# Softmax attention's output product as seven half-size products, in two parts around the linear attention's first half

## The chip, the cores and the metric

The kernel runs on one core of one Trainium2 chip. The metric is the time of one execution on the device, in microseconds (us); the median of 3 runs before the change is 1637.56 us. Engines are named as in the profile: PE is the matrix engine (PEld its weight loads), DVE the vector engine, ACT the scalar engine, POOL the GpSimd engine, and SP the queue from which every DMA of this kernel is issued, in one order.

## The reference

One layer of an encoder block, float32, one batch of 1024 tokens, width 1024:

```python
h = _rms_norm(x, norm_mix_g[l])
proj = h @ w_in[l]
(g_q, g_k, g_v, g_r, g_lr_f, g_lr_b,
 s_q, s_k, s_v, gate_a, gate_b) = jnp.split(proj, split_at, axis=-1)
y_gla = _gla_branch(...) @ w_o_gla[l]      # linear attention, norm, swish gate by g_r
y_swa = _swa_branch(...) @ w_o_swa[l]      # softmax attention in a window of 128
merged = jax.nn.sigmoid(gate_a) * y_gla + jax.nn.sigmoid(gate_b) * y_swa
x = x + merged @ w_out[l]
h2 = _rms_norm(x, norm_ffn_g[l])
gu = h2 @ w_ffn_in[l]
x = x + (jax.nn.silu(gu[..., :D_FF]) * gu[..., D_FF:]) @ w_ffn_out[l]
```

The change concerns `y_swa`'s product with `w_o_swa` (1024 x 1024 by 1024 x 1024 tokens), and the place where the gates `gate_a` and `gate_b` get their factor of the first norm, 1/rms(x) of each token.

## The kernel before

Activations lie with features on the 128 partitions and tokens along the free axis. A tile is 128 x 512: one eighth of the features (index `k` or `m`, 0 to 7) for one half of the tokens (index `s`, 0 or 1). Float32 accuracy comes from splitting each operand into a high part (`h`, rounded by ACT's copy to fp32r) and a low part (`l`, the rest, a subtraction on DVE), and from three matmuls for each 128 x 128 block: high by high, high by low, low by high (`mm3`, and `product` for four blocks in a row). So a half-size product, four blocks deep, is 12 matmuls of 512 columns for each output tile.

Weights come in units of 128 x 512 (four blocks). `wunit` loads one to `wr` (4 buffers), splits it to `wh` on ACT and `wl` on DVE (5 buffers each). `wsplit` does the split alone, for units that are sums of others.

PE's instructions run in the order of the source. The order on DVE, ACT and SP is set by the framework's scheduler: among what it takes to be ready, what comes first in the source goes first. Each of these queues then runs in that fixed order, and an instruction that waits holds up those behind it.

Stages of the time line: projections of the input (0 to 346 us; from 88 us on a part made of seven half-size products per pair of output features, with the gates as its first eight pairs, `pairs[0]` to `pairs[7]`); linear attention (346 to 557 us) and softmax attention (to 740 us), both interleaved with the remaining projections; then the branch products, which the change touches; then the two feed-forward products (from about 1010 us), also by seven half-size products.

The gates' stage: `x_two`, `x_four` and `x_last` make three quarters of each pair's output on DVE (`xc`, `xu`) and hand them to `out_quarter`, which stores them to DRAM (`keep`). The remaining quarter (`ga`, first token half) was stored earlier, by `keep_raw` in `x_first`.

The branch stage before, from 740 us on, in PE's order:

1. `branch_b(0)`: `y_swa`'s product for the first token half, 8 groups of 24 matmuls (`hgroup`), on the split tiles `obh`, `obl` that `prep_b(0)` made during the last of the softmax attention. Each group ends with a product by its gate on DVE, into `xg[m][s]`.
2. `prep_a(0)` (no PE work): for each `k` two DMA loads (`lo`, the linear attention's output, and `lr`, its swish gate's input; two buffers each), a sigmoid on ACT (`sg`, one buffer), two products on DVE, and the split into `oah`, `oal`. `prep_b(1)`: the second half's `ob` tiles.
3. `branch_a(0)`: `y_gla`'s product, 8 groups, each times its gate, plus `xg`, then split into `mh`, `ml`.
4. `branch_b(1)`, `prep_a(1)`.
5. `out_proj(0)`: the product with `w_out` for the first token half, 8 groups; then `branch_a(1)`, and `out_proj(1)`.

`gate` loads a gate's tile, multiplies it by `rstd` on DVE (L1123) and takes the sigmoid on ACT (L1124). PSUM has 8 banks: 4 of tag `mm` and 4 of tag `ch`; before the change all groups of this stage use `mm`.

Of the kernel before, what the change touches and what calls it, by code (L numbers as in the profile page):

```python
# [24 lines left out]
NG = 8  # L25
# [5 lines left out]
def body(tc, i, out):  # L31
    nc = tc.nc
    with ExitStack() as root:
        dram = root.enter_context(tc.tile_pool(name="scr", bufs=1, space=bass.MemoryType.DRAM))
        cst = root.enter_context(tc.tile_pool(name="cst", bufs=1))
        wp = root.enter_context(tc.tile_pool(name="wp", bufs=1))
# [18 lines left out]
        def scratch(name, shape=(P, 512)):  # L55
            return dram.tile(list(shape), F32, tag=name, name=name)
# [21 lines left out]
        def mm3(o, ah, al, bh, bl, start, stop):  # L78
            mm(o, ah, bh, start, False)
            mm(o, ah, bl, False, False)  # L80
            mm(o, al, bh, False, stop)
# [10 lines left out]
        rstd = cst.tile([P, T], F32, tag="rstd", name="rstd")  # L92
# [22 lines left out]
        scr = {}  # L115
# [179 lines left out]
        def wsplit(src, n):  # L295
            h = wp.tile([P, n], FR, tag="wh", name=nm("wh"), bufs=5)
            l = wp.tile([P, n], FR, tag="wl", name=nm("wl"), bufs=5)
            nc.scalar.activation(h, src, AF.Copy)  # L298
            nc.vector.tensor_tensor(l, src, h.bitcast(F32), op=ALU.subtract)  # L299
            return h, l  # L300

        def product(o, w, x, nk, start, stop):
            h, l = w
            for kk in range(nk):
                c = slice(kk * P, (kk + 1) * P)
                nc.tensor.matmul(o, h[:, c], x[kk][0], start=start and kk == 0, stop=False, skip_group_check=True)  # L306
                nc.tensor.matmul(o, h[:, c], x[kk][1], start=False, stop=False, skip_group_check=True)  # L307
                nc.tensor.matmul(o, l[:, c], x[kk][0], start=False, stop=kk == nk - 1, skip_group_check=True)  # L308

        def keep(name, s, t):  # L310
            d = scratch(f"{name}_{s}")
            nc.sync.dma_start(out=d[:t.shape[0]], in_=t)
            scr[name, s] = d
# [38 lines left out]
        def out_quarter(F, b, s, t, src=None):  # L352

            if F.scales:
                nc.vector.scalar_tensor_tensor(t, t if src is None else src, F.scales[b], rstd[:, s * HT:(s + 1) * HT],
                                               op0=ALU.mult, op1=ALU.mult)
            elif src is not None:
                nc.scalar.copy(t, src)
            keep(F.names[b], s, t)

        def x_first(f):
# [179 lines left out]
        with tc.manual_schedule(engines={mybir.EngineType.PE}):  # L541
# [8 lines left out]
            for k in range(KT):  # L550
# [5 lines left out]
                c = slice((k % 4) * P, (k % 4 + 1) * P)  # L556
# [7 lines left out]
            bl = [chtile((P, 512)), chtile((P, 512))]  # L564
# [9 lines left out]
            for f in range(0, NG, 2):  # L574
                x_first(f)
                if f == 0:
                    for s in range(2):
                        v = chtile((P, HT))
# [253 lines left out]
        for n in range(NH * NC):  # L832
            hd, c = divmod(n, NC)
# [173 lines left out]
        def btile(tag, dt=F32, bufs=None):  # L1007
            return (btb if tag in ("lo", "gb") else bta).tile([P, HT], dt, tag=tag, name=nm(tag), bufs=bufs)

        oa, ob, mh, ml = {}, {}, {}, {}  # L1010

        def split_in(o, name, k):
            pool = bob if name == "ob" else boa
            h = pool.tile([P, HT], FR, tag=f"{name}h{k}", name=nm(name + "h"))
            l = pool.tile([P, HT], FR, tag=f"{name}l{k}", name=nm(name + "l"))
            nc.scalar.activation(h, o, AF.Copy)
            nc.vector.tensor_tensor(l, o, h.bitcast(F32), op=ALU.subtract)
            return h, l

        def prep_b(s):  # L1020
            ob[s] = []
            for k in range(KT):
                o = btile("lo")
                nc.sync.dma_start(out=o, in_=scr["b", k, s])
                ob[s].append(split_in(o, "ob", k))

        todo = [[] for _ in range(2 * KT + 6)]
        for n in range(2 * KT):
            g, t = divmod(n, KT)
# [13 lines left out]
        with tc.manual_schedule(engines={mybir.EngineType.PE}):  # L1043
            for t, v in enumerate(todo):
                v.sort(key=lambda e: order.index(e[0]))
                if t == 2 * KT + 3:

                    swas.close()
                    wq = root.enter_context(tc.tile_pool(name="wq", bufs=1))
                    bob = bs.enter_context(tc.tile_pool(name="bob", bufs=1))  # L1050
# [12 lines left out]
        xg = [[x1s.tile([P, HT], F32, tag=f"xg{m}{s}", name=f"xg{m}{s}") for s in range(2)] for m in range(KT)]  # L1063
# [27 lines left out]
        bm = bms.enter_context(tc.tile_pool(name="bm", bufs=1, side="right"))  # L1091
        boa = bs.enter_context(tc.tile_pool(name="boa", bufs=1))
        bta = bs.enter_context(tc.tile_pool(name="bta", bufs=2))

        def hgroup(w, u0, ah, al):
            b = mmtile()
            for u in range(2):
                h, l = wunit(w[u0, u])
                for kk in range(4):
                    k = u * 4 + kk  # L1100
                    c = slice(kk * P, (kk + 1) * P)
                    mm3(b, h[:, c], l[:, c], ah[k], al[k], k == 0, k == KT - 1)
            return b

        acc = fi.tile([P, T], F32, tag="acc", name="acc2")
        def prep_a(s):
            oa[s] = []
            for k in range(KT):
                o = btile("lo")
                nc.sync.dma_start(out=o, in_=scr["o", k, s])  # L1110
                r = btile("lr")
                nc.sync.dma_start(out=r, in_=scr[f"r{k}", s])
                sg = btile("sg", bufs=1)
                nc.scalar.activation(sg, r, AF.Sigmoid)
                nc.vector.tensor_tensor(r, r, sg, op=ALU.mult)
                nc.vector.scalar_tensor_tensor(o, o, og[:, k % 2:k % 2 + 1], r, op0=ALU.mult, op1=ALU.mult)
                oa[s].append(split_in(o, "oa", k))

        def gate(nme, s):
            g = btile(nme[:2])  # L1120
            nc.sync.dma_start(out=g, in_=scr[nme, s])
            if int(nme[2:]) < NG:
                nc.vector.tensor_tensor(g, g, rstd[:, s * HT:(s + 1) * HT], op=ALU.mult)  # L1123
            nc.scalar.activation(g, g, AF.Sigmoid)  # L1124
            return g

        def branch_b(s):

            for m in range(KT):
                g = gate(f"gb{m}", s)  # L1130
                y = hgroup(i["w_ob"], m, [v[0] for v in ob[s]], [v[1] for v in ob[s]])
                nc.vector.tensor_tensor(xg[m][s], y, g, op=ALU.mult)

        def branch_a(s, between=None):
            for m in range(KT):
                if between and m == 3:
                    between()
                g = gate(f"ga{m}", s)
                y = hgroup(i["w_oa"], m, [v[0] for v in oa[s]], [v[1] for v in oa[s]])
                nc.vector.tensor_tensor(g, y, g, op=ALU.mult)  # L1140
                nc.vector.tensor_tensor(g, g, xg[m][s], op=ALU.add)
                h = bm.tile([P, HT], FR, tag=f"mh{m}", name=nm("mh"))
                l = bm.tile([P, HT], FR, tag=f"ml{m}", name=nm("ml"))
                nc.scalar.activation(h, g, AF.Copy)
                nc.vector.tensor_tensor(l, g, h.bitcast(F32), op=ALU.subtract)
                mh[m], ml[m] = h, l

        def out_proj(s):
            a = acc[:, s * HT:(s + 1) * HT]
# [16 lines left out]
        def out_stats(s):  # L1166
            v = chtile((P, HT))
            mm(v, ones, acc[:, s * HT:(s + 1) * HT], True, True)
            rsqrt(rstd[:, s * HT:(s + 1) * HT], v, 1.0 / T, EPS, epst, fi, (P, HT), "rs")

        with tc.manual_schedule(engines={mybir.EngineType.PE}):
            branch_b(0)
            prep_a(0)
            prep_b(1)
            branch_a(0)
            branch_b(1)
            prep_a(1)
            out_proj(0)
            branch_a(1, lambda: out_stats(0))
# [33 lines left out]
        def ctile(tag):  # L1213
            t = x1s.tile([P, HT], F32, tag="xg" + home[tag][turn[tag] % len(home[tag])], name=nm(tag))
            turn[tag] += 1
            return t
# [171 lines left out]
        with tc.manual_schedule(engines={mybir.EngineType.PE}):  # L1388
# [19 lines left out]
            for f in range(NFF):  # L1408
                if f == NFF - 1:
                    for k in range(2):  # L1410
                        r = ctile("oc")
# [140 lines left out]
```

## Time and profile before

| | |
|---|---|
| median of 3 runs | 1637.56 us (1637.46 to 1638.46) |
| the profiled execution's own time | 1637.04 us |
| its span, first to last instruction | 1635.3 us |
| granted PE clock | 1.000 |
| busy: PE, PEld, DVE, ACT, POOL | 1624.3, 1345.4, 1259.9, 813.4, 76.4 us |
| first matmul of `branch_b(0)`, of `branch_a(0)` | 740.0, 783.5 us |
| DMA | 264.49 MB, mean 162 GB/s |

In the profile, L76 is the matmul inside `mm3` (through `mm`), L306 to L308 the three matmuls of `product`, L70 and L72 the split of a weight unit in `wunit`, L1016 and L1017 the split of an activation tile, L1110 and L1112 the loads of `prep_a`, L1114 to L1116 its sigmoid and products, L1132 a group's product by its gate in `branch_b`. SPq is the SP queue. The matmuls are pipelined, so the duration of one (389 ns) is longer than the distance from one to the next.

### The profile page before, as it was taken

The numbers are of one execution on the slowest core, as the hardware profiler recorded it, in microseconds if no ns is written. First come the engines' busy times: TensorE is split into PE (matmuls) and PEld (weight loads), VectorE is DVE, ScalarE is ACT, GpSimd is POOL, SyncE is SP. The second block draws the span as 40 slices with busy tenths as digits, with TensorE's granted clock in tenths as the row PEclk, the third lists the DMA queues.
The fourth block names the chain that finished last, engine by engine and source line by source line (L and its number), as shares of the span: only waits on it lengthen the run. The fifth ranks groups of instructions, "written<-read, shape, count | busy, mean of one in ns | idle before, by whom it ended". The sixth has DMA issues, their size and how long they took to land.

```text
span 1635.3 us, 23259 instructions
## 1 busy us (share of the span) xinstructions
PE 1624.3 (99%) x7588; PEld 1345.4 (82%) x7588; DVE 1259.9 (77%) x2627; ACT 813.4 (50%) x1666; POOL 76.4 (5%) x68
## 2 busy tenths in 40 slices
PE   9999999999999999999999999999999999999999
PEld 7888888888888778888888888888888888888887
DVE  8866665589998499868785679887777788779655
ACT  8622224466787577665544547333333333354442
POOL 0000000000000045440000000000000000000000
PEclk9999999999999999999999999999999999999999
DMA  7554334486554633248665554443234443596433
GB/s 242 175 179 148 116 115 143 160 270 180 164 175 147 193 115 104 85 161 279 212 206 180 155 165 131 149 149 115 99 115 142 146 144 130 186 336 195 150 98 117
DMA packets 172170, 264.49 MB, mean 162 GB/s; under 512 B 23484, under 2 KB 57020, under 8 KB 172048
## 3 DMA queue, kind: packets, MB, share of 16 engines
q1 hardware_dynamic: 172048, 262.99, 50.2%
q8 instruction: 60, 0.98, 0.2%
q14 instruction: 62, 0.51, 0.1%
HBM read 188.45 MB, written 74.47 MB: 161 GB/s over the span
## 4 chain that ended last, share of the span: by engine, by line
PE 85%; DVE 10%; ACT 3%; DMA 1%; issue 1%; SPq 0%; DVEq 0%; ACTq 0%
PE mm L76 23%; PE mm L306 9%; PE mm L308 9%; PE mm L307 9%; PE mm L1365 7%; PE ch L1365 5%; PE ch L76 4%; PE ch L308 4%; PE ch L307 4%; PE ch L306 4%; PE ch L460 3%; PE mm L460 2%; DVE cs L655 1%; DVE wl L72 1%; PE ch L988 1%
## 5 line engine op out<-in xcount | busy, mean ns | idle before, releaser
L298 ACT ACTIVATE wh<-ws 128x512 fp32r<-128x512 f32 x132 | 83.3, 632 | 196.4 <-PE mm L307 104.6
L70 ACT ACTIVATE wh<-wr 128x512 fp32r<-128x512 f32 x202 | 125.0, 627 | 92.3 <-PE mm L76 53.5
L72 DVE TENSOR_TENSOR wl<-wr,wh 128x512 fp32r<-128x512 f32 x202 | 137.5, 686 | 26.0 <-ACT wh L70 25.6
L299 DVE TENSOR_TENSOR wl<-ws,wh 128x512 fp32r<-128x512 f32 x132 | 90.6, 686 | 22.8 <-ACT wh L298 22.7
L977 POOL TENSOR_SCALAR p<-p,rd 128x384 f32<-128x384 f32 (+1 forms) x64 | 76.2, 1207 | 648.4 <-DMA kvr<-skv 585.3
L298 ACT ACTIVATE wh<-wr 128x512 fp32r<-128x512 f32 x69 | 43.6, 632 | 125.1 <-issue 49.7
L298 ACT ACTIVATE wh<-a 128x512 fp32r<-128x512 f32 x64 | 40.5, 633 | 90.5 <-PE mm L1365 42.4
L76 PE MATMUL mm<-wh,xl 128*128 128x512 f32 x192 | 83.1, 433 | 0.0
L76 PE MATMUL mm<-wh,xh 128*128 128x512 f32 x192 | 79.7, 415 | 0.0
L76 PE MATMUL mm<-wl,xh 128*128 128x512 f32 x192 | 79.5, 414 | 0.0
L299 DVE TENSOR_TENSOR wl<-a,wh 128x512 fp32r<-128x512 f32 x64 | 44.2, 691 | 42.3 <-ACT wh L298 41.8
L1365 PE MATMUL mm<-hh,wh 128*128 128x512 f32 x176 | 68.5, 389 | 0.0
L1365 PE MATMUL mm<-hl,wh 128*128 128x512 f32 x176 | 68.5, 389 | 0.0
L1365 PE MATMUL mm<-hh,wl 128*128 128x512 f32 x176 | 68.5, 389 | 0.0
L76 PE MATMUL mm<-xh,wh 128*128 128x512 f32 x160 | 64.5, 403 | 0.3 <-ACT wh L70 0.3
L76 PE MATMUL mm<-xl,wh 128*128 128x512 f32 x160 | 64.5, 403 | 0.0
L76 PE MATMUL mm<-xh,wl 128*128 128x512 f32 x160 | 59.8, 408 | 0.0
L1335 DVE TENSOR_TENSOR hl<-hr,hh 128x512 fp32r<-128x512 f32 x75 | 51.4, 686 | 4.4 <-ACT hh L1334 4.4
L1365 PE MATMUL ch<-hh,wh 128*128 128x512 f32 x132 | 51.3, 389 | 0.0
L1365 PE MATMUL ch<-hl,wh 128*128 128x512 f32 x132 | 51.3, 389 | 0.0
L1365 PE MATMUL ch<-hh,wl 128*128 128x512 f32 x132 | 51.3, 389 | 0.0
L76 PE MATMUL mm<-oah,wh 128*128 128x512 f32 x128 | 50.2, 392 | 0.0
(617 smaller groups left out, 5054.6 us busy)
## 6 DMA issues: line engine op xcount, KB each, us to landing
wr<-in_w_fi_dram SPq DMA_DIRECT2D x102, 256.0 KB
wr<-in_w_f_dram SPq DMA_DIRECT2D x80, 256.0 KB
wr<-in_w_t_dram SPq DMA_DIRECT2D x56, 256.0 KB
B<-c SPq DMA_DIRECT2D x44, 256.0 KB
T<-tx SPq DMA_DIRECT2D x44, 256.0 KB
a<-in_w_fo_dram SPq DMA_DIRECT2D x44, 256.0 KB
hr<-T SPq DMA_DIRECT2D x44, 256.0 KB
wr<-in_w_ob_dram SPq DMA_DIRECT2D x32, 256.0 KB
```

What stands on the lines that cost most here:

```text
L70: nc.scalar.activation(h, raw, AF.Copy)
L72: nc.vector.tensor_tensor(l, raw, h.bitcast(F32), op=ALU.subtract)
L76: nc.tensor.matmul(o, a, b, start=start, stop=stop)
L298: nc.scalar.activation(h, src, AF.Copy)
L299: nc.vector.tensor_tensor(l, src, h.bitcast(F32), op=ALU.subtract)
L306: nc.tensor.matmul(o, h[:, c], x[kk][0], start=start and kk == 0, stop=False, skip_group_check=True)
L307: nc.tensor.matmul(o, h[:, c], x[kk][1], start=False, stop=False, skip_group_check=True)
L308: nc.tensor.matmul(o, l[:, c], x[kk][0], start=False, stop=kk == nk - 1, skip_group_check=True)
L460: nc.tensor.matmul(ys[m], a[:, c], b, start=f0, stop=f1, skip_group_check=True)
L977: nc.gpsimd.tensor_scalar(p[:, h, :w], p[:, h, :w], rd[:, h:h + 1], None, op0=ALU.mult)
L1335: nc.vector.tensor_tensor(l, r, h.bitcast(F32), op=ALU.subtract)
L1365: nc.tensor.matmul(ys[m], a[:, c], b, start=f0, stop=f1, skip_group_check=True)
```

## The change

The product for `y_swa` is taken for both token halves at once, as a 2 x 2 block product (output features by tokens, four tiles to a block) with seven half-size products in place of eight, in Winograd's form. `b_first`, ahead of `branch_a(0)`, makes two of them (weights 11 by activations 11, and weights 12 by activations 21) and finishes the first output quarter; the first product stays in the four `mm` banks (`A`). `b_raw` loads both halves' unsplit activations and makes the sums; `b_rest`, after `branch_a(0)`, makes the other five, on sums of weights made on DVE. `branch_a(0)` runs in the `ch` banks, and for `m` over 3 its result waits in `xg[m][0]` and is merged inside `b_rest`. `branch_b` goes; `prep_b(1)` goes; `prep_a(1)` now follows `b_rest`, whose activations lie in the tiles of `oa`. Besides, in the gates' stage `out_quarter` multiplies the three quarters by `rstd`, and `gate` keeps that product only for `ga` of the first token half.

```diff
@@ out_quarter
             elif src is not None:
                 nc.scalar.copy(t, src)
+            else:
+                nc.vector.tensor_tensor(t, t, rstd[:, s * HT:(s + 1) * HT], op=ALU.mult)
             keep(F.names[b], s, t)
@@ hgroup
-        def hgroup(w, u0, ah, al):
-            b = mmtile()
+        def hgroup(w, u0, ah, al, bank=mmtile):
+            b = bank((P, HT))
@@ gate
-            if int(nme[2:]) < NG:
+            if nme[1] == "a" and s == 0:
                 nc.vector.tensor_tensor(g, g, rstd[:, s * HT:(s + 1) * HT], op=ALU.mult)
             nc.scalar.activation(g, g, AF.Sigmoid)
             return g
 
-        def branch_b(s):
-
-            for m in range(KT):
-                g = gate(f"gb{m}", s)
-                y = hgroup(i["w_ob"], m, [v[0] for v in ob[s]], [v[1] for v in ob[s]])
-                nc.vector.tensor_tensor(xg[m][s], y, g, op=ALU.mult)
+        def merged(m, g):
+            h = bm.tile([P, HT], FR, tag=f"mh{m}", name=nm("mh"))
+            l = bm.tile([P, HT], FR, tag=f"ml{m}", name=nm("ml"))
+            nc.scalar.activation(h, g, AF.Copy)
+            nc.vector.tensor_tensor(l, g, h.bitcast(F32), op=ALU.subtract)
+            mh[m], ml[m] = h, l
@@ branch_a
-                y = hgroup(i["w_oa"], m, [v[0] for v in oa[s]], [v[1] for v in oa[s]])
+                y = hgroup(i["w_oa"], m, [v[0] for v in oa[s]], [v[1] for v in oa[s]], mmtile if s else chtile)
+                if s == 0 and m > 3:
+                    nc.vector.tensor_tensor(xg[m][0], y, g, op=ALU.mult)
+                    continue
                 nc.vector.tensor_tensor(g, y, g, op=ALU.mult)
                 nc.vector.tensor_tensor(g, g, xg[m][s], op=ALU.add)
...
+                merged(m, g)
+
+        bx, bw = {}, {}
+
+        def bw_load(m, u, ring):
+            t = wp.tile([P, 512], F32, tag="wr", name=nm("bw"), bufs=4) if ring == "wr" else \
+                wq.tile([P, 512], F32, tag="wr2", name=nm("bw"), bufs=3)
+            nc.sync.dma_start(out=t, in_=i["w_ob"][m, u])
+            return t
+
+        def bset(q, k, src, pool, h, l):
+            h = pool.tile([P, HT], FR, tag=h, name=nm("bh"))
+            l = pool.tile([P, HT], FR, tag=l, name=nm("bl"))
+            nc.scalar.activation(h, src, AF.Copy)
+            nc.vector.tensor_tensor(l, src, h.bitcast(F32), op=ALU.subtract)
+            bx.setdefault(q, []).append((h, l))
+
+        def b_raw(k):
+
+            r = []
+            for t, kk, s in ((f"obh{k}", k, 0), (f"obl{k}", k, 1), (f"obl{k + 4}", k + 4, 0), (f"obh{k + 4}", k + 4, 1)):
+                o = bob.tile([P, HT], F32, tag=t, name=nm("br"))
+                nc.sync.dma_start(out=o, in_=scr["b", kk, s])
+                r.append(o)
+            b11, b12, b21, b22 = r
+            nc.vector.tensor_tensor(b12, b12, b11, op=ALU.subtract)
+            nc.vector.tensor_tensor(b22, b22, b12, op=ALU.subtract)
+            bset("T2", k, b22, bm, f"mh{k + 4}", f"ml{k + 4}")
+            nc.vector.tensor_tensor(b11, b22, b11, op=ALU.subtract)
+            nc.vector.tensor_tensor(b21, b21, b22, op=ALU.subtract)
+            bx["raw", k] = b11, b12, b21
+
+        def b_first():
+            bx["11"], bx["21"] = ob[0][:4], ob[0][4:]
+            A = [mmtile() for _ in range(4)]
+            p = []
+            for m in range(4):
+                product(A[m], wunit(i["w_ob"][m, 0]), bx["11"], 4, True, False)
+                p.append(bm.tile([P, HT], F32, tag=f"mh{m + 4}", name=nm("bp")))
+                nc.scalar.copy(p[m], A[m])
+            for m in range(4):
+                g = gate(f"gb{m}", 0)
+                y = chtile((P, HT))
+                product(y, wunit(i["w_ob"][m, 1]), bx["21"], 4, True, True)
+                nc.vector.tensor_tensor(p[m], y, p[m], op=ALU.add)
+                nc.vector.tensor_tensor(xg[m][0], p[m], g, op=ALU.mult)
+            return A
+
+        def b_rest(A):
+            s1, s2 = [], []
+            for m in range(4):
+                a21, a22 = bw_load(m + 4, 0, "wr"), bw_load(m + 4, 1, "wr2")
+                t = wq.tile([P, 512], F32, tag="ws", name=nm("bs1"), bufs=4)
+                nc.vector.tensor_tensor(t, a21, a22, op=ALU.add)
+                s1.append(t)
+                a11 = bw_load(m, 0, "wr")
+                t = bob.tile([P, 512], F32, tag=f"obh{m + 4}", name=nm("bs2"))
+                nc.vector.tensor_tensor(t, s1[m], a11, op=ALU.subtract)
+                s2.append(t)
+                product(A[m], wsplit(t, 512), bx["T2"], 4, False, False)
+                nc.scalar.copy(xg[m][1], A[m])
+                bset("T1", m, bx["raw", m][1], boa, f"oah{m}", f"oal{m}")
+            for m in range(4):
+                product(A[m], wsplit(s1[m], 512), bx["T1"], 4, False, False)
+                nc.scalar.copy(xg[m + 4][1], A[m])
+                bset("T3", m, bx["raw", m][0], bm, f"mh{m + 4}", f"ml{m + 4}")
+                bset("T4", m, bx["raw", m][2], boa, f"oah{m + 4}", f"oal{m + 4}")
+            C = [chtile((P, HT)) for _ in range(4)]
+            for m in range(4):
+                a11, a21 = bw_load(m, 0, "wr"), bw_load(m + 4, 0, "wr2")
+                nc.vector.tensor_tensor(a11, a11, a21, op=ALU.subtract)
+                product(C[m], wsplit(a11, 512), bx["T3"], 4, True, False)
+                g = gate(f"gb{m + 4}", 1)
+                nc.vector.tensor_tensor(xg[m + 4][1], C[m], xg[m + 4][1], op=ALU.add)
+                nc.vector.tensor_tensor(xg[m + 4][1], xg[m + 4][1], g, op=ALU.mult)
+                o = btile("lo")
+                nc.sync.dma_start(out=o, in_=scr["b", m + 4, 1])
+                bset("22", m, o, boa, f"oah{m}", f"oal{m}")
+            for m in range(4):
+                product(C[m], wunit(i["w_ob"][m + 4, 1]), bx["T4"], 4, False, True)
+                g, c = gate(f"gb{m + 4}", 0), xg[m][1]
+                nc.vector.tensor_tensor(c, C[m], c, op=ALU.add)
+                nc.vector.tensor_tensor(c, c, g, op=ALU.mult)
+                nc.vector.tensor_tensor(c, c, xg[m + 4][0], op=ALU.add)
+                merged(m + 4, c)
+            for m in range(4):
+                a12 = bw_load(m, 1, "wr")
+                nc.vector.tensor_tensor(a12, a12, s2[m], op=ALU.subtract)
+                product(A[m], wsplit(a12, 512), bx["22"], 4, False, True)
+                g = gate(f"gb{m}", 1)
+                nc.vector.tensor_tensor(xg[m][1], A[m], g, op=ALU.mult)
@@ order of the branch stage
-            branch_b(0)
+            A = b_first()
             prep_a(0)
-            prep_b(1)
+            for k in range(4):
+                b_raw(k)
             branch_a(0)
-            branch_b(1)
+            b_rest(A)
             prep_a(1)
             out_proj(0)
             branch_a(1, lambda: out_stats(0))
```

More of the change, by code (lines that the diff above doesn't have):

```diff
@@ L1138, in branch_a @@
                 g = gate(f"ga{m}", s)
-                y = hgroup(i["w_oa"], m, [v[0] for v in oa[s]], [v[1] for v in oa[s]])
+                y = hgroup(i["w_oa"], m, [v[0] for v in oa[s]], [v[1] for v in oa[s]], mmtile if s else chtile)
+                if s == 0 and m > 3:
+                    nc.vector.tensor_tensor(xg[m][0], y, g, op=ALU.mult)
+                    continue
                 nc.vector.tensor_tensor(g, y, g, op=ALU.mult)
                 nc.vector.tensor_tensor(g, g, xg[m][s], op=ALU.add)
-                h = bm.tile([P, HT], FR, tag=f"mh{m}", name=nm("mh"))
@@ L1143, in branch_a @@
[L1143 to L1146, printed above, removed]
+                merged(m, g)
[5 more added lines that the diff above has]
+            return t
```

## Prediction

> **What bounds the kernel now.** I read the page first: busy times, the clock, and the chain of work that ended last.
>
> ```profile
> span 1635.3 us, 23259 instructions
> PE 1624.3 (99%) x7588; PEld 1345.4 (82%) x7588; DVE 1259.9 (77%) x2627; ACT 813.4 (50%) x1666; POOL 76.4 (5%) x68
> PEclk9999999999999999999999999999999999999999
> PE 85%; DVE 10%; ACT 3%; DMA 1%; issue 1%; SPq 0%; DVEq 0%; ACTq 0%
> ```
>
> PE bounds it: 85% of the chain, at full clock. But busy time cannot say whether PE is at its rate, since matmuls overlap. So next the chain in order of time, where a piece is a stretch in which nothing but PE's own order held it.
>
> ```profile
> 250.09 10.88 PE ch L460 x48
> 732.43 198.13 PE mm L76 x874
> ```
>
> 48 matmuls in 10.88 us, and 874 in 198.13 us, are both 226.7 ns apiece. The second piece covers all of the branch stage: from 732 to 930 us PE never waits. So a matmul taken out there is worth 226.7 ns, and any wait put in costs its full length. Then a table by stage: `branch_b(0)` in two halves, `branch_a(0)`, `branch_b(1)`, `out_proj(0)`; the gates' stage; and, for comparison, the busiest stretch of DMA that I found. The columns are busy us (and instructions) of PE, PEld, DVE, ACT, POOL, the clock, the busy share of the DMA engines, and GB/s.
>
> ```profile
> core 0: us, PE busy (x) PEld busy (x) DVE busy (x) ACT busy (x) POOL busy (x), PEclk, DMA share, GB/s
> 740.00:761.80 21.80, 21.80 (x98) 18.06 (x97) 19.42 (x31) 12.30 (x22) 0.00 (x0) 1.00 0.87 279
> 761.80:783.50 21.70, 21.70 (x97) 17.98 (x96) 18.13 (x30) 12.30 (x23) 0.00 (x0) 1.00 0.84 260
> 783.50:827.00 43.50, 43.50 (x193) 36.03 (x192) 33.27 (x53) 21.67 (x39) 0.00 (x0) 1.00 0.62 199
> 827.00:870.60 43.60, 43.60 (x194) 36.08 (x194) 36.07 (x57) 21.38 (x39) 0.00 (x0) 1.00 0.66 208
> 870.60:914.20 43.60, 43.60 (x194) 36.12 (x193) 23.74 (x37) 22.62 (x38) 0.00 (x0) 1.00 0.62 187
> 88.00:197.00 109.00, 108.22 (x478) 89.27 (x477) 72.56 (x114) 29.55 (x49) 0.00 (x0) 1.00 0.44 146
> 1421.00:1467.00 46.00, 46.00 (x205) 38.09 (x204) 35.76 (x57) 24.13 (x41) 0.00 (x0) 1.00 0.99 354
> ```
>
> PE is hidden behind nothing, but in the first 43.5 us DVE and the DMA engines are both at 86% or so: there `prep_a(0)` runs beside `branch_b(0)`.
>
> **The matmuls: -10.88 us.** `branch_b` has 2 x 8 groups of 24, 384 matmuls. After: `b_first` 8 products of 12, `b_rest` 20 of 12, 336. 48 fewer x 226.7 ns = 10.88 us. This is a ceiling: nothing else in the change shortens PE's work.
>
> **The join of `b_first` and `branch_a(0)`: +7.0 us.** `prep_a(0)` used to have `branch_b(0)`'s 43.5 us as cover; it now has `b_first`'s 96 matmuls, 21.8 us. The rows: the first matmuls on `ob` and `oa` tiles, and the DVE instructions that finish `oal` for k = 1 and 7 of the first token half and k = 2 and 7 of the second.
>
> ```profile
> L76 PE MATMUL mm<-obh,wh x128: 389/389/389, 740.0 to 869.9; 128*128 128x512 f32 x128
> L76 PE MATMUL mm<-oah,wh x128: 389/389/793, 783.5 to 957.8; 128*128 128x512 f32 x128
> 747.03 0.68 DVE L1017 TENSOR_TENSOR oal<-lo,oah 128x512 fp32r<-128x512 f32 x1
> 774.94 0.69 DVE L1017 TENSOR_TENSOR oal<-lo,oah 128x512 fp32r<-128x512 f32 x1
> 836.50 0.68 DVE L1017 TENSOR_TENSOR oal<-lo,oah 128x512 fp32r<-128x512 f32 x1
> 855.07 0.68 DVE L1017 TENSOR_TENSOR oal<-lo,oah 128x512 fp32r<-128x512 f32 x1
> ```
>
> `b_first` ends at 740.0 + 21.8 = 761.8. The first group of `branch_a(0)` takes its eight `oa` tiles in order, 3 matmuls each; the eighth `oal` is read by its 23rd matmul, at 761.8 + 22 x 0.2267 = 766.8. At the pace of before it is done at 774.94 + 0.69 = 775.6. So PE, which did not wait, would wait 8.8 us in that first group, and all later PE work moves by that. The pace is 4.65 us per k, (774.94 - 747.03) / 6; it is not a price of work but of a chain with two buffers (load, sigmoid, two products, split) whose every step queues behind others on SP, ACT and DVE. Two things move it.
>
> DVE's queue, from 740 to 775 us, by line (busy us, mean ns | idle us ahead of it and its cause):
>
> ```profile
> L1132 DVE TENSOR_TENSOR xg<-mm,gb 128x512 f32<-128x512 f32 x5 | 3.4, 685 | 0.0
> L1123 DVE TENSOR_TENSOR gb<-gb,rstd 128x512 f32<-128x512 f32 x4 | 2.8, 693 | 2.4 <-DMA gb<-gb 2.4
> ```
>
> The four `gb` products go, and with them the 2.4 us in which DVE stood in line for their loads: 5.2 us. In place of five group products come eight (an addition and a product for each of four groups): 3 x 0.685 = 2.1 us. Net -3.1 us. The four copies of `A` on ACT, at the 0.63 us of the sigmoid quoted below, lie in the 9.5 us that ACT is idle in 740 to 761.8.
>
> The loads: `b_raw` stands ahead of `branch_a(0)` in the source and its first eight tiles come free when the first four products end, near 751 us, the other eight near 761.8. Each is 256 KB, 0.74 us at the 354 GB/s of the last row of the table; 16 take 11.8 us. The spare share in 740 to 783.5 is 13% of 21.8 and 16% of 21.7, 6.3 us. So at worst 5.5 us of loads go ahead of `prep_a(0)`'s last ones; at best none. How long a load takes when it meets others is seen at k = 3:
>
> ```profile
> 748.11 0.42 SPq L1112 DMA_DIRECT2D lr<-r  x1
> 753.74 0.63 ACT L1114 ACTIVATE sg<-lr 128x512 f32<-128x512 f32 x1 [1.10 <-DMA lr<-r]
> ACT sg L1114 <- DMA lr<-r: 9.4, 8, 2.3
> ```
>
> 5.6 us from issue to use, though the waits that this made on ACT are 9.4 us over 8 times, 1.2 us each. I take one such wait: +1.2, with 0 and +5.5 as ends. Sum: 8.8 - 3.1 + 1.2 = 6.9, taken as 7.0 us. The low end is the pace at which the second token half's tiles were made, under a DMA share of 0.66: (855.07 - 836.50) / 5 = 3.7 us per k, so the eighth at 747.03 + 6 x 3.7 + 0.69 = 769.9, a wait of 3.1 us; zero if DVE's relief comes on top. The high end is 8.8 + 5.5 = 14.3 us.
>
> The Trainium skill's page DMA: Bandwidth & Descriptors (Anatomy of one DMA) gives a load, on another queue path than this one, as about 2.0 us and its bytes at 436 GB/s: an estimate of 2.6 us for 256 KB. With that and the four steps behind it a buffer would turn in about 5.4 us, 2.7 per k, `oal` would be whole at 764 us, and the join would cost nothing. The 5.6 us above, under load, speaks against it; the rival "join hidden" stands without it.
>
> **DVE in `b_rest`: +0.8 us.** Successive DVE products of this size start 0.60 us apart:
>
> ```profile
> 782.81 1.29 DVE L1017 TENSOR_TENSOR obl<-lo,obh 128x512 fp32r<-128x512 f32 x2
> ```
>
> (two in 1.29 us, the last being 0.69 long). Per product of 2.72 us on PE the five loops of `b_rest` carry 4, 3, 5, 5 and 3 of them: 2.4, 1.8, 3.0, 3.0, 1.8 us. Loops three and four overdraw by 4 x 2 x 0.28 = 2.2 us; the units split ahead (five `wl`) cover that, and loop five pays it back. From 740 us to the end of `b_rest` I count 180 DVE instructions (`b_first` 16, `prep_a(0)` 24, `b_raw` 20, `branch_a(0)` 40, `b_rest` 80), 108 us of 119.7 us of PE work, 90%; before, the table's rows give 19.42 + 18.13 + 33.27 + 36.07 = 106.9 us busy of 130.6, 82%. The ends: 0 if the five units hold, 5 us if a tenth of `b_rest`'s 48 us of DVE is lost to waits in line. I take 0.8, near the low end, because the nearest row, 740.00:761.80, has DVE busy 89% and PE unheld.
>
> **Edits costed at nothing.** Loads: 16 more in all (8 raw tiles, 4 reloads for "22", 36 weight units for 32), 11.8 us of DMA; the three stages have about 36 us of spare share, and `b_rest`'s loop one, three loads in 2.72 us (2.2 us of DMA), can load ahead into `wr2` and `ws`. SP: 16 issues of 0.33 us. ACT: 20 splits and 12 copies more, 8 splits fewer, 24 x 0.63 = 15 us, beside 63 us idle in the three stages. PSUM: each bank of `A` or `C` is read four products (10.9 us) before it is written again; `branch_a(0)` has the four `ch` banks. `prep_a(1)` moves behind `b_rest`, since its tiles hold `b_rest`'s activations: 24 DVE products and 16 loads go into `out_proj(0)`, making 61 x 0.60 = 37 of 43.6 us on DVE and about 0.9 of the DMA; at 4.65 us per k it ends after some 33 us, ahead of `branch_a(1)`, with 10 us over. If that cover is gone, the first group of `branch_a(1)` waits as the first of `branch_a(0)` does. The gates' stage gets 24 products, 14.4 us of DVE beside 36 us of idle time in 109; what is late next is only the stores, read 500 us later. The 24 products taken from `gate` were on no PE path.
>
> **Sum.** Against the profiled execution's own 1637.04 us: -10.88 + 7.0 + 0.8 = -3.1, 1634.0 us. That execution is 0.5 us under the median, 1637.56; I leave the number at 1634.0, which is 0.2% under the median. 0.2%, 3.3 us, is about what a measurement of this kernel can tell from no change: faster is under 1634.3, slower over 1640.8. So the forecast sits on the edge.
>
> **Rivals.**
>
> *The join is hidden.* For: DVE's relief, and 3.7 us per k in the second half. Against: the first half's own 4.65. Wait 0 to 3.1, tail 0 to 0.8: 1626.2 to 1630.1 us.
>
> *The wait eats the gain.* The change does what it says, and the wait of 8.8 us stays as it was paced, with some 2 us of the tail: 1637.04 - 10.88 + 8.8 + 2 = 1637.0. For it: DVE's `b_raw` sums can stand in line where `gb` did.
>
> *The loads collide, and it is slower.* One mechanism, at 751 to 775 us: `b_raw`'s 16 loads go out as their tiles come free, ahead of `prep_a(0)`'s loads for k = 4 to 7, whose two buffers let only two be asked for at once. Wait 14.3, tail 0.8: 1641.3 us. It decides when the wait passes 10.88 + 3.8 = 14.7 less the tail, about 13.9. For it: the share is 0.87 already. Against: it needs all the burst in front and none of DVE's relief.
>
> *DVE overdrawn in `b_rest`*, the upper end of that term on top of the forecast: 1634.0 + 4.2 = 1638.2.
>
> **How the numbers follow.** Forecast (1631 to 1637) 0.42, a little over half of it under the edge; join hidden 0.18; gain eaten 0.13; loads collide, from there upwards, 0.17; DVE overdrawn 0.10, a part of it with a long join and so over 1640.8. Faster 0.18 + 0.24 = 0.42; slower 0.17 + 0.05 = 0.22; same the rest, 0.36. The range leaves one in ten on either side: 1628 to 1642.5. The forecast's own range is 1631 to 1637.
>
> **What would show it.** The matmul count in the branch stage is 48 lower at 226.7 ns. Right: one gap of about 7 us in PE near 762 to 775 us, ended by a split of `lo` on DVE (`oal`), and no other over 1 us up to `branch_a(1)`. In `prep_a(0)`, `oal` for k = 7 near 774 us; `lr` and `lo` loads landing later than before if the burst matters. Wrong: `oal` whole by 768 us (join hidden), or past 780 (loads); pieces of the chain on DVE inside `b_rest`; a gap at the first group of `branch_a(1)`; any gap in the gates' stage beyond the one at 88 us.

## The result and the profile after

The changed kernel takes 1645.41 us (median of four runs, 1644.42 to 1647.12) against 1637.51 us for the kernel before on the same chip: a ratio of 1.0049, interval 1.0031 to 1.0066, 7.9 us slower. The forecast was 1634.0 and its range ended at 1642.5. The profiled execution took 1644.84 us, its span 1643.1.

From the page of the changed kernel: span, busy times, granted clock by fortieths of the span, and shares of the chain that ended last.

```profile
span 1643.1 us, 23240 instructions
PE 1616.4 (98%) x7540; PEld 1339.5 (82%) x7540; DVE 1288.4 (78%) x2679; ACT 823.5 (50%) x1686; POOL 76.3 (5%) x68
PEclk9999999999999999998999999999999999999999
PE 83%; DVE 10%; ACT 4%; DMA 2%; issue 1%; SPq 0%; DVEq 0%; ACTq 0%
```

PE is busy 7.9 us less and the span is 7.8 us longer. There are 48 PE records fewer, as many as the matmuls that went. The clock has one slice under 9, the nineteenth, 739 to 780 us: there the branch stage begins. What PE waited for on other engines between 755 and 885 us is one line (us in total, times, longest):

```profile
PE ch L76 <- DVE wl L72: 15.3, 1, 15.3
```

A single wait of 15.3 us, and not for `oal`: for `wl`, the low part of a weight unit. PE's order around it (start, us, instruction, idle time before it and what ended it):

```profile
765.61 0.39 PE L76 MATMUL ch<-oal,wh 128*128 128x512 f32 x1
781.30 0.79 PE L76 MATMUL ch<-oah,wl 128*128 128x512 f32 x1 [15.31 <-DVE wl L72]
781.90 0.63 PE L76 MATMUL ch<-oah,wh 128*128 128x512 f32 x1
782.32 0.63 PE L76 MATMUL ch<-oal,wh 128*128 128x512 f32 x1
```

It is the second unit of `branch_a(0)`'s first group: PE got through the first unit, `oa` tiles 0 to 3, and stopped. The high part of the second unit was ready from 756.29 + 0.62 us; for its low part, here is ACT's row and then DVE's queue:

```profile
756.29 0.62 ACT L70 ACTIVATE wh<-wr 128x512 fp32r<-128x512 f32 x1
```

```profile
771.54 0.69 DVE L1019 TENSOR_TENSOR oal<-lo,oah 128x512 fp32r<-128x512 f32 x1
772.14 0.69 DVE L1161 TENSOR_TENSOR bl<-br,bh 128x512 fp32r<-128x512 f32 x1
772.74 0.69 DVE L1175 TENSOR_TENSOR br<-br,br 128x512 f32<-128x512 f32 x1
...
779.97 0.68 DVE L1173 TENSOR_TENSOR br<-br,br 128x512 f32<-128x512 f32 x1
780.57 0.68 DVE L72 TENSOR_TENSOR wl<-wr,wh 128x512 fp32r<-128x512 f32 x1
```

The `oal` at 771.54 is that of k = 7. Behind it DVE does `b_raw`'s sums and splits (`br`, `bl`), which `b_rest` reads first at 823 us: fourteen of its twenty instructions, one every 0.60 us and without idle time, 8.4 us. Only at 780.57 comes the `wl` for which PE stands. (Three more of the twenty stand further ahead, three behind.) The unit's load had been issued at 745.39 us, and its high part was there, so no load held it. Nothing in that queue is slow. The cause is its order, which in the main follows the source, and the source puts `b_raw` ahead of `branch_a(0)`.

The stretch by windows (columns as before: PE, PEld, DVE, ACT, POOL, clock, DMA share, GB/s); first of the changed kernel, then of the kernel before.

```profile
755.00:785.00 30.00, 14.69 (x58) 11.71 (x57) 27.64 (x46) 13.07 (x22) 0.00 (x0) 0.77 0.87 299
765.00:781.00 16.00, 1.00 (x5) 0.49 (x3) 14.97 (x25) 7.00 (x12) 0.00 (x0) 0.70 0.97 346
781.30:785.00 3.70, 3.69 (x9) 2.92 (x10) 3.70 (x7) 1.16 (x3) 0.00 (x0) 0.50 0.48 159
823.50:877.90 54.40, 54.40 (x241) 45.08 (x240) 45.17 (x74) 32.38 (x60) 0.00 (x0) 1.00 0.56 167
```

```profile
755.00:785.00 30.00, 30.00 (x134) 24.86 (x133) 25.43 (x41) 16.23 (x29) 0.00 (x0) 1.00 0.82 255
```

DVE is busy 92% of 755 to 785 us; before it was 85%, with PE never held. The granted clock falls during the wait (second row: 0.70 on the mean), and PE is granted half for 3.7 us after it resumes: nine matmuls about 0.43 us apart instead of 0.227, 9 x 0.2 = 1.8 us more. The last row is `b_rest`: 240 matmuls at 226.7 ns are 54.4 us, and that is its length.

The starts of three stages, before in the prediction's rows, after here:

```profile
L306 PE MATMUL mm<-obh,wh x16: 389/389/390, 740.9 to 751.1; 128*128 128x512 f32 x16
L76 PE MATMUL ch<-oah,wh x64: 388/390/629, 762.7 to 822.8; 128*128 128x512 f32 x64
L76 PE MATMUL mm<-mh,wh x128: 389/389/390, 877.9 to 1008.7; 128*128 128x512 f32 x128
```

The account: the branch stage starts 0.9 us late (740.9 for 740.0); `b_first` lasts 21.8, as forecast; `branch_a(0)` lasts from 762.7 to 823.5, 60.8 us instead of 43.5: +17.3, of which 15.3 the wait, 1.8 the clock, 0.2 unassigned; `b_rest` loses nothing. `out_proj(0)` starts at 877.9 instead of 870.6, +7.3 = 0.9 - 10.9 + 17.3, and 0.5 more is lost up to the end of the span.

### The profile page after: what moved, and what is told of

It reads as the page before. It is cut to its first block, busy times and chain, and to the rows that moved or that the text cites. A ratio compares the mean times of both kernels' runs of the same rounds, so it can differ in the third digit from the quotient of the medians.

```text
span 1643.1 us, 23240 instructions
## 1 busy us (share of the span) xinstructions
PE 1616.4 (98%) x7540; PEld 1339.5 (82%) x7540; DVE 1288.4 (78%) x2679; ACT 823.5 (50%) x1686; POOL 76.3 (5%) x68
## 4 chain that ended last, share of the span: by engine, by line
PE 83%; DVE 10%; ACT 4%; DMA 2%; issue 1%; SPq 0%; DVEq 0%; ACTq 0%
PE mm L76 17%; PE mm L306 9%; PE mm L308 9%; PE mm L307 9%; PE ch L76 7%; PE mm L1457 7%; PE ch L1457 5%; PE ch L308 4%; PE ch L306 4%; PE ch L307 4%; PE ch L462 3%; PE mm L462 2%; DVE wl L72 1%; PE ch L990 1%; DVE p L959 1%
## 5 line engine op out<-in xcount | busy, mean ns | idle before, releaser
L70 ACT ACTIVATE wh<-wr 128x512 fp32r<-128x512 f32 x182 | 112.9, 628 | 86.8 <-PE mm L76 44.1
L72 DVE TENSOR_TENSOR wl<-wr,wh 128x512 fp32r<-128x512 f32 x182 | 123.8, 684 | 21.1 <-ACT wh L70 20.9
L298 ACT ACTIVATE wh<-wr 128x512 fp32r<-128x512 f32 x69 | 43.6, 633 | 124.8 <-issue 49.7
L1457 PE MATMUL ch<-hh,wl 128*128 128x512 f32 x132 | 51.4, 389 | 0.0
L1457 PE MATMUL ch<-hh,wh 128*128 128x512 f32 x132 | 51.4, 389 | 0.0
L1457 PE MATMUL ch<-hl,wh 128*128 128x512 f32 x132 | 51.4, 389 | 0.0
L76 PE MATMUL mm<-mh,wh 128*128 128x512 f32 x128 | 49.8, 389 | 0.0
```

Source lines behind the costliest of these rows:

```text
L76: nc.tensor.matmul(o, a, b, start=start, stop=stop)
L1457: nc.tensor.matmul(ys[m], a[:, c], b, start=f0, stop=f1, skip_group_check=True)
```

## The experiments

My theory was the order on DVE: PE waits for whatever stands behind `b_raw` in that queue. The rivals were the loads of `b_raw` on SP (eight of them, 4.12 us of issuing, stand ahead of the loads of `w_oa`), and `prep_a(0)` with too little cover. The kernel before took 1637.4 to 1637.7 us beside each of them, and each ratio is to it. Several of the early expectations had the mechanism right and the numbers wrong.

**e1: `b_raw` one group later.** `branch_a` gets a parameter for the place of its call.

```
-            for k in range(4):
-                b_raw(k)
-            branch_a(0)
+            branch_a(0, lambda: [b_raw(k) for k in range(4)], 1)
```

> Edit: b_raw for all four k moves from ahead of branch_a(0) to behind its first group; nothing else. Order theory (the 15.3 us wait of PE at the join is the low part of branch_a(0)'s second weight unit, which stands on DVE behind b_raw's sums, and these behind b_raw's loads): the wait falls to what oal for k = 7 asks, done at 772.2 us against 767.65 needed, so about 4.6 us; no drop of the granted clock, or a shorter one; 15.5 - 4.6 = 10.9 us less and some 1.9 us of slow clock less than the 1645.4 of the change: 1632 to 1635 us. Rival, pace of prep_a(0): the two-buffer chain is late by itself once the weights are not, the wait stays over 8 us, 1637 us or more. Rival, loads collide: with b_raw's loads behind the first group's, oal for k = 7 is done before 769, the wait is under 2 us, 1630 us or less.

1648.89 us, 1.0065 (1.0053 to 1.0078): no better, and far over what the order theory gave. The time lies where the rival on `prep_a(0)`'s pace put it, but that rival's long wait was to end on `oal`, and this one again ends on `wl`. PE's wait moved from the second unit of the first group to the second group:

```profile
785.84 0.79 PE L76 MATMUL ch<-oah,wl 128*128 128x512 f32 x1 [11.36 <-DVE wl L72]
```

and the first group now waited 2.8 us for `oah` and `oal`. So the wait goes where `b_raw` goes; one group of cover is not enough for it.

**e2: the kernel before, with the gates' products moved alone.** The branch functions are as before; `out_quarter` and `gate` are as in the change.

```
+            else:
+                nc.vector.tensor_tensor(t, t, rstd[:, s * HT:(s + 1) * HT], op=ALU.mult)
...
-            if int(nme[2:]) < NG:
+            if nme[1] == "a" and s == 0:
```

> Edit: the kernel before, with the move of the norm's product from gate to out_quarter alone. Order theory: it is on no path of PE; 1637.5 us within 1 us either way. Rival: the 0.9 us by which the changed kernel starts its branch stage later (733.33 against 732.43 us) comes from this move, through the longer DVE queue of the gates' stage or the changed order at the first sigmoid: 1638.4 us.

1638.34 us, 1.0004 (0.9995 to 1.0013): no difference that can be measured. In its profile the branch stage starts at 741.0, as in the changed kernel, but e11 below has the gates' move too and starts it at 740.0, as the kernel before does:

```profile
L306 PE MATMUL mm<-obh,wh x16: 389/389/389, 740.0 to 750.2; 128*128 128x512 f32 x16
```

So the 0.9 us is not shown to be the gates' part. It lies within this interval, and neither of the two expectations can be told from the other.

**e3: e1, and `prep_a(0)` ahead of `b_first`.**

```
-            A = b_first()
             prep_a(0)
+            A = b_first()
+            branch_a(0, lambda: [b_raw(k) for k in range(4)], 1)
```

> Edit: as the kernel with b_raw behind the first group, and prep_a(0) also moved ahead of b_first in the source, so that its steps go first on DVE, ACT and SP. Order theory: oal for k = 7 is done 1 to 4 us earlier, the wait at the join falls to 1 to 4 us, 1629 to 1633 us. Rival: the source order matters little here since the two-buffer chain waits for loads, the time stays within 1 us of the kernel without this move. Second rival: b_first's own weight units now stand behind prep_a(0) and PE waits inside b_first, 2 to 5 us slower than the kernel without this move.

1647.84 us, 1.0059 (1.0046 to 1.0071). `oal` for k = 7 was ready at 767.9 us and nothing waited for it any more; still the time barely moved from e1's. PE waited 7.2 us for `wh` and 7.6 for `wl` instead. In this order the loads have a part too: the units asked for at 770.72 us stand on SP behind eight loads of `b_raw`, and the high part that PE waited for was split only at 776.25.

```profile
765.63 4.08 SPq L1169 DMA_DIRECT2D br<-b  x8
...
770.72 2.47 SPq L68 DMA_DIRECT2D wr<-in_w_oa_dram  x4
```

`prep_a(0)`'s lack of cover is therefore not what holds this kernel while `b_raw` stands near the front.

**e4: the first four units of `w_oa` fetched and split ahead of `b_raw`**, which stays in place.

```
             prep_a(0)
+            pre += [wunit(i["w_oa"][n // 2, n % 2]) for n in range(4)]
             for k in range(4):
                 b_raw(k)
```

> Edit: the changed kernel, b_raw in its place, but the first four weight units of branch_a(0) are loaded and split ahead of b_raw in the source. Order theory: the wait at the join falls to that of oal, 4 to 6 us; b_raw's sums now stand ahead of the fifth unit (third group), done near 783 us, which PE asks for near 778, so up to 5 us more there: 1634 to 1640 us. Rival, loads collide: b_raw's 16 loads still go out ahead, so oal or the units stay late, the waits together stay over 12 us, 1641 us or more. Rival, pace of prep_a(0): one wait over 8 us that ends on oal, 1637 to 1640 us.

1643.94 us, 1.0036 (1.0023 to 1.0048), over the 1634 to 1640 of the order theory. The first four units no longer wait; 4.4 us of waits on `oah` and `oal` appear, and the fifth unit, the first behind `b_raw`, waits:

```profile
787.78 0.80 PE L76 MATMUL ch<-oah,wl 128*128 128x512 f32 x1 [5.18 <-DVE wl L72]
```

**e5 and e6: loads against sums.** e5 leaves `b_raw`'s loads where they are and puts its DVE and ACT work behind `branch_a(0)`; e6 puts loads and sums behind it, both in the order of the source.

```
 e5:             branch_a(0)
     +            for k in range(4):
     +                b_sums(k)
                  b_rest(A)
 e6:             prep_a(0)
     +            branch_a(0)
                  for k in range(4):
                      b_raw(k)
     -            branch_a(0)
                  b_rest(A)
```

> Edit: the changed kernel with b_raw cut in two: its 16 loads stay ahead of branch_a(0) in the source, its 16 sums and the four T2 splits move behind branch_a(0), ahead of b_rest. DVE theory (from 755 to 785 us DVE is busy 92 to 95% in every order tried so far, and the next weight unit's low part comes at 780 to 787 us, once all b_raw sums are through; moving b_raw by one group or putting units ahead only moves the wait to the next unit): with the sums out of that stretch the wait of 11 to 15 us is gone, waits on oal of 3 to 5 us in all stay, the clock stays at 1.00, 1630 to 1634 us. Rival, SP's order: the units' loads still stand behind b_raw's loads (issued at 770 to 772 us in all four orders), so PE then waits for the high part or the load of a unit, 7 us or more in all: 1635 to 1640 us.

> Edit: the changed kernel with all of b_raw, loads and sums, behind branch_a(0) in the source. DVE theory and SP's order agree here on the join: waits on oal of 1 to 5 us, clock 1.00, 1629 to 1633 us. They part from the kernel with loads early and sums late: if that one is equal within 1.5 us, DVE alone made the wait; if this one is faster by 3 us or more, SP's order had its share. Rival: the sums now crowd the end of branch_a(0) and PE waits at the start of b_rest instead, 5 us or more, 1636 us or more.

e5: 1636.58 us, 0.9993 (0.9984 to 1.0002). e6: 1636.01 us, 0.9990 (0.9981 to 0.9999). The long wait is gone in both, and they differ by 0.6 us, less than either interval is wide, so the loads on SP were no part of it; the sums on DVE were. Both times are above what was forecast for the sums on DVE, and e5's lies in the range of the rival on SP; its waits decide against that rival, since none is on the high part of a weight unit and 0.2 us on a low part. What PE still waits for in e6 between 755 and 885 us, the window around it, and the split of the unit for which PE had stood:

```profile
PE ch L76 <- ACT oah L1018: 3.2, 2, 2.7
PE ch L76 <- DVE oal L1019: 0.9, 2, 0.5
...
765.00:785.00 20.00, 15.97 (x55) 11.38 (x54) 18.09 (x30) 8.89 (x16) 0.00 (x0) 0.83 0.89 298
...
759.11 0.68 DVE L72 TENSOR_TENSOR wl<-wr,wh 128x512 fp32r<-128x512 f32 x1
```

That split runs 21 us earlier than in the changed kernel. The sums do not wait for the end of `branch_a(0)`: the first of them runs at 773.96 us, among its work. What the order of the source moved is the place of the split in DVE's queue.

`branch_a(0)` lasts 51.4 us in e6, 7.9 more than its 43.5: 4.1 in these waits, some 1.8 in nine matmuls at half the clock, the rest in smaller gaps. This is the join without `b_raw` in it.

**e7: e6, and `prep_a(0)` ahead of `b_first`.**

```
-            A = b_first()
             prep_a(0)
-            for k in range(4):
-                b_raw(k)
+            A = b_first()
             branch_a(0)
+            for k in range(4):
+                b_raw(k)
```

> Edit: all of b_raw behind branch_a(0), and prep_a(0) ahead of b_first in the source. In the earlier run with prep_a(0) ahead, oal for k = 7 was done at 767.9 us and PE never waited on oal. Theory: the last waits of the join go, 1628 to 1631 us, 1 to 4 us faster than with b_raw last alone. Rival: b_first's own units come late instead, no gain or 1 to 2 us slower than with b_raw last alone.

1630.87 us, 0.9960 (0.9947 to 0.9972): faster than both kernels, and as expected. The window from 755 to 785 us, then PE's waits up to 885 us:

```profile
755.00:785.00 30.00, 29.24 (x127) 23.36 (x126) 28.18 (x46) 14.37 (x25) 0.00 (x0) 1.00 0.93 306
...
PE ch L76 <- DVE oal L1019: 0.6, 1, 0.6
PE mm L306 <- ACT wh L298: 0.6, 1, 0.6
```

DVE is fuller than in the changed kernel, 94%, and PE is hardly held: the fill did not decide, the order did. `branch_a(0)` takes 1.7 us more than its matmuls need, `b_rest` 1.4, and the stage starts 0.7 late; `out_proj(0)` begins at 863.4, 7.2 us ahead of before.

**e8: e7 without the gates' move**, so that the norm products of the other 24 gates are done in `gate` again.

```
-            else:
-                nc.vector.tensor_tensor(t, t, rstd[:, s * HT:(s + 1) * HT], op=ALU.mult)
...
-            if nme[1] == "a" and s == 0:
+            if int(nme[2:]) < NG:
```

> Edit: b_raw behind branch_a(0) and prep_a(0) ahead of b_first, as in the fastest so far (1630.9 us), but the norm's product back in gate: the second part of the change undone. If DVE's load in the branch stage is what makes the join and b_rest wait (DVE 28.2 of 30 us from 755 to 785 us), 16 products of gb there, of which four before 766 us, cost PE 2 to 4 us, less the 0.7 us by which the stage starts earlier: 1632 to 1635 us. Rival: the waits that are left (0.6 us on oal, 0.6 on a unit) are not DVE's load, and the move only costs its 0.7 to 0.9 us ahead of the stage: 1630 us, the same or faster by under 1 us.

1644.20 us, 1.0040 (1.0027 to 1.0053): 13.3 us over e7, far more than I expected. PE's waits (11.0 us in all, 1.2 in e7), and the window in which the longest of them lies:

```profile
PE mm L76 <- DVE wl L72: 5.6, 1, 5.6
PE ch L76 <- DVE wl L72: 3.8, 1, 3.8
PE mm L308 <- DVE wl L299: 1.6, 1, 1.6
...
825.00:880.00 55.00, 47.87 (x201) 38.67 (x200) 49.82 (x82) 28.43 (x50) 0.00 (x0) 0.94 0.57 180
```

All three are for low parts of weights on DVE: the 3.8 us at 769 us in `branch_a(0)`, the 1.6 at 865 in `b_rest`, the 5.6 at 874 near the start of `out_proj(0)`. My reading, which no run isolates, is that the products put back go into a queue that has 10.88 us less PE time to cover it. The move that measured as nothing by itself (e2) is worth 13.3 us here.

**e9: e7, with `b_raw`'s sixteen sums on POOL.**

```
-            nc.vector.tensor_tensor(b12, b12, b11, op=ALU.subtract)
+            nc.gpsimd.tensor_tensor(b12, b12, b11, op=ALU.subtract)
...
```

> Edit: the fastest so far (b_raw behind branch_a(0), prep_a(0) ahead of b_first) with the 16 sums of b_raw on POOL, which is idle there, in place of DVE; the T2 splits stay on DVE. If DVE's load is what is left of the waits: the 0.6 us at the start of b_rest and part of the 1.7 us lost in the join go, 1629 to 1630.5 us. Rival: the sums are slower on POOL (a 128x384 product takes 1.2 us there) or hold up DVE while they run, the T2 splits then stand in DVE's queue for them: 1632 us or more.

1644.35 us, 1.0044 (1.0033 to 1.0056): 13.5 us over e7, within the 1632 or more that the rival gave. Groups by line between 768 and 804 us, e9 first, then e7:

```profile
L1161 DVE TENSOR_TENSOR bl<-br,bh 128x512 fp32r<-128x512 f32 x3 | 4.7, 1583 | 4.6 <-ACT bh L1160 4.6
L72 DVE TENSOR_TENSOR wl<-wr,wh 128x512 fp32r<-128x512 f32 x10 | 10.4, 1055 | 2.4 <-ACT wh L70 2.4
L1145 DVE TENSOR_TENSOR ga<-ch,ga 128x512 f32<-128x512 f32 x3 | 2.0, 678 | 0.0
L1176 POOL TENSOR_TENSOR br<-br,br 128x512 f32<-128x512 f32 x4 | 6.9, 1724 | 0.0
```

```profile
L72 DVE TENSOR_TENSOR wl<-wr,wh 128x512 fp32r<-128x512 f32 x14 | 9.4, 683 | 0.2 <-ACT wh L70 0.2
```

DVE was spared sixteen instructions and made slower in those beside them, 1055 ns on the mean for `wl` instead of 683. The product that reads PSUM (`ch`) kept its 678 ns. DVE also stood 4.6 us for a split that waits for POOL's sums, and how the 13.5 us divide between the two is not shown.

**e10: e7, and six more gates' products moved.** The first half's `ga2` to `ga7` leave `x_first` multiplied by `rstd` on DVE, instead of copied by ACT, and `gate` multiplies `ga0` and `ga1` alone.

```
-                keep_raw(f"ga{f + j}", 0, Y[j])
+                if f:
+                    c = ep.tile([P, HT], F32, tag="c", name=nm("c"), bufs=2)
+                    nc.vector.tensor_tensor(c, Y[j], rstd[:, 0:HT], op=ALU.mult)
+                    keep(f"ga{f + j}", 0, c)
+                else:
+                    keep_raw(f"ga{f + j}", 0, Y[j])
```

> Edit: the fastest so far (b_raw behind branch_a(0), prep_a(0) ahead of b_first; 1630.9 us), and six of the eight ga products of the first token half also leave the branch stage: x_first stores ga2 to ga7 as DVE's product with rstd in place of ACT's copy. If what is left of the loss (1.7 us in the join, 1.4 at b_rest) is DVE's load, 3.6 us of DVE less from 745 to 806 us takes 0.5 to 2 us off: 1629 to 1630.5 us. Rival: DVE is not what is left there, or the six products cost PE something in the first stage: 1630.5 to 1632 us.

1628.91 us, 0.9949 (0.9936 to 0.9961): the fastest of all, 8.7 us under before. The 2.0 us to e7 are less well shown, since the two intervals overlap; the profile agrees with them, with no wait of PE left from 735 to 1015 us. Its window, and the start of `out_proj(0)`:

```profile
755.00:785.00 30.00, 29.90 (x131) 24.09 (x130) 28.06 (x46) 14.44 (x26) 0.00 (x0) 1.00 0.93 310
...
L76 PE MATMUL mm<-mh,wh x128: 389/389/389, 861.7 to 992.5; 128*128 128x512 f32 x128
```

**e11: e7, with `b_raw` ahead of the sixth group of `branch_a(0)`** instead of behind the last.

```
-            branch_a(0)
-            for k in range(4):
-                b_raw(k)
+            branch_a(0, lambda: [b_raw(k) for k in range(4)], 5)
```

> Edit: the fastest so far, with b_raw ahead of the sixth group of branch_a(0) in place of behind the eighth. Order theory: far enough behind the join, the T2 splits come sooner, the 0.6 us wait at the start of b_rest goes, 1629.5 to 1631 us. Rival: what is put ahead of a group's units in the source makes the units late, as it did at the second group: PE waits there 2 us or more with the slow clock behind it, 1633 us or more.

1636.08 us, 0.9995 (0.9986 to 1.0004), 5.2 us over e7. I had expected that five groups of cover would do; they do not, and the rival written beside it held:

```profile
796.38 0.50 PE L76 MATMUL ch<-oah,wl 128*128 128x512 f32 x1 [2.94 <-DVE wl L72]
```

Ahead of the first, second, third and sixth group (the changed kernel, e1, e4, e11), PE waits at the first `wl` behind `b_raw`: 15.3, 11.4, 5.2 and 2.9 us. (The last has `prep_a(0)` early, as e3, where the wait ahead of the second group was 6.6.) Of the places tried, only the one with no group behind it is without the wait.

## Why the prediction was wrong, by its steps

- **-10.88 us of matmuls: right.** `b_first` took 21.8 us and `b_rest` 54.4, each what its matmuls make at 226.7 ns.
- **The join, +7.0: the step that failed.** It measured +17.3. The part that was worked out, `prep_a(0)` with 21.8 us of cover, was right in kind: `oal` for k = 7 was ready at 771.54 + 0.69 = 772.2 us, where 774 was forecast; PE, starting at 762.7, wanted it at 767.7, a wait of 4.6 where the term had 7.0; and e6, the join without `b_raw`, has waits of 4.1. That e6 loses 7.9 in all, near the 7.0, is luck: 1.8 of it is the clock, which the sum did not have. What was left out is `b_raw` on DVE: 17.3 - 7.9 = 9.4 us of the loss. The term took `b_raw` as 16 loads, with 14.3 as its worst, and its 20 DVE instructions went only into an average, 108 of 119.7 us over the stage. But seventeen of them stood ahead of the low part of the second unit of `w_oa`, fourteen in one piece behind `prep_a(0)`'s last split, 14 x 0.60 = 8.4 us in a queue that cannot pass them by. The prediction even named it, under "the wait eats the gain" ("DVE's `b_raw` sums can stand in line where `gb` did"), and priced it by the old 8.8 us instead of by the queue.
- **The rival "the loads collide" had the right sign (1641.3, where 1645.4 was measured) and nearly the wait (14.3 for 15.3), with the wrong mechanism, which is luck**: between e5 and e6 the place of the loads makes 0.6 us.
- **The clock after the wait, +1.8 us, was not in the sum at all**, though it came here with waits of 15.3 us (the changed kernel) and of 2.9 (e11), and with e6's cluster.
- **DVE in `b_rest`, +0.8: it measured 0.** It was 0 too in e10, where no wait stood in front of it, and 1.4 in e7, of which 0.6 is a wait for a high part on ACT. So the runs do not bear the term out.
- **The gates' move at nothing: right by itself, wrong as a part.** It stood in the text as "on no PE path". Alone it measured as nothing (e2). As relief of the branch stage it is worth 13.3 us once the order is mended (e8).
- **"What would show it wrong" missed as well**: it listed `oal` too late and DVE inside `b_rest`, not `wl` inside `branch_a(0)`.

Open: where the 0.9 us at the start comes from; the 0.7 us that e10 still loses from 763.1 to 861.7 (98.6 us for 97.9 of matmuls); how much of e7's gain over e3 is the sums and how much the loads, which moved together; and whether e10's gain over e7, 2.0 us, comes from DVE's relief in the branch stage alone, since it also takes six copies off ACT earlier.

## What to carry to other kernels

Work that a stage needs late, put early into an in-order queue, is priced by what stands behind it: go through the queue of each engine in its order, and ask of each item on PE's path what is ahead of it (here 8.4 us of sums and splits, behind the tail of `prep_a(0)`, kept a 0.68 us split until PE had waited 15.3 us; without them the waits were 4.1). An average fill over a stage says little: DVE 92% full cost 17.3 us in one order, 94% full 1.7 us in another. And a part of a change that measures as nothing by itself can be what carries the rest, so try it with and without in the version that works.

## What the runs showed of the hardware

- **A stop of PE cost more here than its length.** Over the 16 us from 765 to 781 us, the wait of the changed kernel, the granted clock was 0.70: one fall from 1.00 to 0.50 makes that with 9.6 us at half, so it fell near 771.4 us, some 5 us after PE had stopped. It was still 0.50 from 781.30 to 785.00 us, and nine matmuls stood about 0.43 us apart. In e6 the same followed a cluster of waits of which the longest was 2.7 us, and in e11 a single wait of 2.9 us (clock 0.78 from 796 to 798 us, 0.50 to 800). In e7, after waits of 0.6 us, the clock stayed at 1.00. The Trainium skill's page TensorE: Matmul & The Clock Gate (Part 1: The HAM clock gate) has the clock fall to half after an idle window of about 3.4 us; the trace agrees in the wait of 15.3 us, and e6 and e11 show it also where no single wait was as long as the page's window.
- **POOL's sums slowed DVE.** In e9, DVE products with both inputs in SBUF went from 0.68 us to as much as 1.7 or 1.8 while a sum ran on POOL, and one with an input in PSUM stayed at 0.68. The Trainium skill's page SBUF — State Buffer (Who interferes with whom) says that a DVE instruction with two SBUF inputs contends with a GpSimd instruction that reads SBUF, since the second input comes through a read interface that the two share; the rows agree.
